# Attention scores of one row of query blocks in a two-bank PSUM tile, with one maximum, one exponential and one sum

## The chip, the cores and the metric

The kernel runs on one core of a Trainium2 chip. The metric is device time in microseconds (us) from launch to end, as the median of three runs. Times of single instructions come from one profiled execution.

## What is computed

Two layers of a decoder trunk, on 1024 tokens of width 1024, in float32. Each layer has a token-mixing sub-layer of four head groups (A, B, C, D) and a gated MLP. The change touches group C, causal softmax attention with four heads:

```python
def attend(args):                      # one block of 128 queries
    qn, qr, blk = args
    sc = (einsum('bqhd,bkhd->bhqk', qn, k_nope)
          + einsum('bqhd,bkd->bhqk', qr, k_rope)) * scale
    q_pos = blk * Q_BLOCK + arange(Q_BLOCK)
    mask = key_pos[None, :] <= q_pos[:, None]
    p = softmax(where(mask, sc, MASK_VALUE), axis=-1)
    return einsum('bhqk,bkhv->bqhv', p, v)
```

Groups A and B are gated linear recurrences, computed chunk by chunk; they share the stretch of the program with group C. Everything else of the reference is left out here, since the change does not touch it.

## The kernel before

`mixing` runs first the input projections and group D, then a stretch in which groups A, B and C are computed together, then the output projection with `w_out`. `ffn` follows. This happens once for each of the two layers. In the middle stretch, called the attention stage below, two streams are interleaved: `group_c` (32 steps, one for each head h and block t of 128 queries) and `ab` (32 steps of `gla_levels`, `gla_chunks` and the head norms of groups A, B and D). The interleaving sets the order in which the work is written; the framework's scheduler then places every instruction on its engine, and each engine keeps to that order.

PSUM has eight banks, each 512 float32 wide on 128 partitions. In the attention stage `PS2` divides them: four single-bank buffers under the tag `cs` (scores), two under `ct` (projections of q and k, transposes, outputs), two under `pm` (groups A and B).

For block t, `scores(h, t)` has (t+1)*128 keys. It is called a row below; rows t = 0 to 3 are short (at most 512 keys, one bank), rows t = 4 to 7 long (two banks). For each piece of up to 512 keys TensorE writes the products q k into one `cs` buffer (two passes of matmul for a float32 piece); on the piece with the diagonal it adds the causal mask by a bf16 matmul of `caus` with an identity. VectorE takes the maximum of each piece (L764). One `tensor_scalar` turns the maxima into the bias of the exponential (L767 for two pieces, L769 for one). ScalarE takes the exponential of each piece (L773) with its sum, which the trace shows as a second instruction, ACTIVATION_READ_ACCUMULATOR. For two pieces VectorE adds the sums (L776); then comes the reciprocal (L778). `apply(h, t)` follows two rows later (`LA = 2`): TensorE transposes P through `ct` (L219 is the transposing helper), ScalarE copies the result to `PT` (L790), TensorE multiplies by v and ScalarE scales by the reciprocal (L794). L215 is the helper that records nearly all other matmuls of the stage, so they are told apart by tiles: `cs` scores, `ct` projections and outputs, `pm` groups A and B.

Of groups A and B the lines named below are: L481 (exponential of a level), L490, L497 and L499 (masked queries of a level), L509 and L511 (copies of a level's products into `at`), L555 and L565 (output and state of a chunk), L480, L483 and L437 on GpSimd. L747 makes Q of the next head.

After the stage `cc` and `g` are closed and the buffers of the weights of `w_out` (L192) are opened in their place.

Of the kernel before, what the change touches and what calls it, by code (L numbers as in the profile page):

```python
# [12 lines left out]
AF = mybir.ActivationFunctionType  # L13
ALU = mybir.AluOpType
AX = mybir.AxisListType
# [113 lines left out]
class Body:  # L129
# [60 lines left out]
    def load(self, src, shape, pool="w", tag="wst", bufs=2):  # L190
        st = self.t(pool, tag, bufs, shape)
        self.nc.sync.dma_start(out=st, in_=src)  # L192
        return st
# [515 lines left out]
    def group_c(self, l, ckv, wv, load, krd, out):  # L709
        nc = self.nc  # L710
        small = lambda sh, tag, bufs=2, dt=F32: self.t("cc", tag, bufs, sh, dt)
        cx = lambda j: load(j, small(None, f"cx{j}", 1))
        wukv = small([128, 256], "wukv", 1)
        nc.sync.dma_start(out=wukv, in_=self.I["wukv"][l, :, 0:256])
        wuq = small([128, 2, 512], "wuq", 1)
        nc.sync.dma_start(out=wuq, in_=self.I["wuq"][l])
        cq = cx(0), cx(1)
        tab = small([128, S], "tab", 1)
        nc.sync.dma_start(out=tab, in_=self.I["tab"])
        vt = [small([128, 4, 256], f"cv{z}", 1) for z in range(2)]  # L720
        for tp in range(4):
            p = self.ps([128, 2, 256], "ct")
            for e in range(2):
                t = tp * 2 + e
                self.mm(p[:, e, :], ckv[:, t * 128:(t + 1) * 128], wv)
            nc.scalar.copy(out=vt[tp // 2][:, (tp % 2) * 2:(tp % 2) * 2 + 2, :], in_=p)

        id16 = small([128, 128], "id16", 1, BF16)
        nc.vector.tensor_copy(out=id16, in_=self.ident)
        caus = small([128, 128], "caus", 1, BF16)  # L730
        nc.vector.tensor_copy(out=caus, in_=self.cf[:, C_CAUS:C_CAUS + 128])
        scale = 96.0 ** -0.5
        QK = {}

        def head(h):
            Q = small(None, "Q", 2)
            K = small(None, "K", 2)
            nc.sync.dma_start(out=K[64:128], in_=krd)
            for n in range(2):
                sl = slice(n * 512, (n + 1) * 512)  # L740
                p = self.ps([64, 512], "ct")
                self.mm(p, wukv[:, h * 64:(h + 1) * 64], ckv[:, sl])
                nc.scalar.copy(out=K[0:64, sl], in_=p)
                p = self.ps([128, 512], "ct")
                for i in range(2):
                    self.mm(p, wuq[:, i, h * 128:(h + 1) * 128], cq[i][:, sl], i == 0, i == 1)
                nc.vector.tensor_tensor(out=Q[:, sl], in0=p, in1=tab[:, sl], op=ALU.mult)  # L747
            QK[h] = Q, K

        def scores(h, t):  # L750
            Q, K = QK[h]
            nk = (t + 1) * 128
            qc = Q[:, t * 128:(t + 1) * 128]
            ps = []
            nm = small([128, 2], "nm", 4)
            for a in range(0, nk, 512):
                e = min(nk, a + 512)
                dg = e == nk
                p = self.ps([128, 512], "cs")[:, 0:e - a]
                self.mm(p, qc, K[:, a:e], True, not dg)  # L760
                if dg:
                    self.mm(p[:, e - a - 128:e - a], id16, caus, False, True)
                i = len(ps)
                nc.vector.tensor_reduce(out=nm[:, i:i + 1], in_=p, axis=AX.X, op=ALU.max)  # L764
                ps.append(p)
            if len(ps) == 2:
                nc.vector.tensor_scalar(out=nm[:, 0:1], in0=nm[:, 0:1], scalar1=nm[:, 1:2], scalar2=-scale, op0=ALU.max, op1=ALU.mult)  # L767
            else:
                nc.vector.tensor_scalar(out=nm[:, 0:1], in0=nm[:, 0:1], scalar1=-scale, scalar2=None, op0=ALU.mult)  # L769
            P = small(None, "P", LA + 1)  # L770
            sm = small([128, 2], "sm", 4)
            for i, p in enumerate(ps):
                nc.scalar.activation(out=P[:, i * 512:i * 512 + p.shape[1]], in_=p, func=AF.Exp, scale=scale, bias=nm[:, 0:1],  # L773
                                     accum_out=sm[:, i:i + 1])
            if len(ps) == 2:
                nc.vector.tensor_tensor(out=sm[:, 0:1], in0=sm[:, 0:1], in1=sm[:, 1:2], op=ALU.add)  # L776
            rc = small([128, 1], "rc", 4)
            nc.vector.reciprocal(out=rc, in_=sm[:, 0:1])  # L778
            return P, rc

        def apply(h, t, P, rc):
            po = None
            PT = small([128, 8, 128], "PT", 2)
            for j in range((t + 4) // 4):
                n = min(4, t + 1 - j * 4)
                p = self.ps([128, 4, 128], "ct")
                for b in range(n):
                    kb = j * 4 + b
                    self.tr(p[:, b, :], P[:, kb * 128:(kb + 1) * 128])
                nc.scalar.copy(out=PT[:, j * 4:j * 4 + n, :], in_=p[:, 0:n, :])  # L790
            po = self.ps([128, 64], "ct")
            for kb in range(t + 1):
                self.mm(po, PT[:, kb, :], vt[kb // 4][:, kb % 4, h * 64:(h + 1) * 64], kb == 0, kb == t)
            nc.scalar.activation(out=out(t)[:, h * 64:(h + 1) * 64], in_=po, func=AF.Copy, scale=rc)  # L794

        head(0)
        prev = []
        for h in range(4):
            for t in range(8):
                prev.append((h, t) + scores(h, t))  # L800
                if t == 4 and h < 3:
                    head(h + 1)
                if len(prev) > LA:
                    apply(*prev.pop(0))
                yield
        for a in prev:
            apply(*a)
# [260 lines left out]
    def mixing(self, l, hT, x_src, x_dst):  # L1068
# [21 lines left out]
        self.exp_ln(self.marks["tanh"])  # L1090
        self.open_ps(**PS2)
        self.open("z", side="left")
# [573 lines left out]
NP, NU, NUL, NFIN = 10, 4, 4, 6  # L1666

LA = 2
PS2 = dict(cs=4, ct=2, pm=2)
NN = (32, 32)  # L1670

HALF = (slice(0, 2), slice(2, 4))
# [25 lines left out]
```

## Time and profile before

| what | value |
|---|---|
| median of 3 runs | 2962.63 us (2961.93 to 2962.8) |
| the profiled execution's own time | 2966.25 us |
| its span, first to last instruction | 2964.5 us |
| PE busy (share of the span) | 2746.8 us (93%) |
| DVE busy | 1868.4 us (63%) |
| ACT busy | 1272.9 us (43%) |
| POOL busy | 1211.7 us (41%) |
| attention stage, layer 0 | about 475 to 698 us |
| attention stage, layer 1 | about 1950 to 2173 us |

PE is TensorE, PEld its weight loads, DVE VectorE, ACT ScalarE, POOL GpSimd, SP the queue that issues the DMAs. Busy shares are means over stages with different limits, so the two attention stages have to be read by themselves. The profiled execution took 3.6 us longer than the median.

### The profile page before, as it was taken

To read this page: it belongs to the slowest core of one execution; us is meant where nothing else is said; L and a number is where in the kernel's file an instruction comes from. 1 tells how busy PE (TensorE), PEld (TensorE's weight loads), DVE (VectorE), ACT (ScalarE), POOL (GpSimd) and SP (SyncE) were. 2 spreads that over 40 slices of the span, in tenths; PEclk is the share of its full clock that TensorE was granted. 3 is DMA by queue.
4 is the path that set the end of the run, shared out by engine and by line. 5 is a ranking of instruction groups with operands and counts; after the bars stand their busy time and mean duration, and the time that the engine had idled before them with its cause. 6 is when DMAs were issued, how large, how long until landed. Compare 5 with 4: busy or idle time off the path is not lost. (4 is left out here: it accounts for less than half of the span.)

```text
span 2964.5 us, 40124 instructions
## 1 busy us (share of the span) xinstructions
PE 2746.8 (93%) x14928; PEld 2230.7 (75%) x14928; DVE 1868.4 (63%) x2726; ACT 1272.9 (43%) x2338; POOL 1211.7 (41%) x1030
## 2 busy tenths in 40 slices
PE   7999898899889999999979998978998999999998
PEld 6787685677777888888767876956776778888887
DVE  5564424893597777764645645258836977777645
ACT  4523335555543333354435233365545433333443
POOL 2122675444575454300231326744446654443001
PEclk9999999999999999999989999999999999999999
DMA  3221764123433223376522226741134332333765
GB/s 115 66 94 57 243 251 160 49 72 107 149 103 110 98 100 105 124 255 194 171 67 69 90 74 234 266 140 57 58 114 149 102 112 101 100 101 105 258 196 192
DMA packets 162675, 386.02 MB, mean 130 GB/s; under 512 B 25488, under 2 KB 37040, under 8 KB 162480
## 3 DMA queue, kind: packets, MB, share of 16 engines
q1 hardware_dynamic: 162480, 383.47, 38.8%
q8 instruction: 117, 1.92, 0.3%
q14 instruction: 78, 0.64, 0.1%
HBM read 273.76 MB, written 109.64 MB: 129 GB/s over the span
## 5 line engine op out<-in xcount | busy, mean ns | idle before, releaser
L209 PE MATMUL pd<-h,wr 128*128 128x512 f32 x2608 | 668.3, 406 | 29.5 <-ACT wr L197 19.8
L198 POOL TENSOR_TENSOR wr<-wst,wr 128x512 fp32r<-128x512 f32 (+1 forms) x184 | 351.1, 1910 | 750.4 <-ACT wr L197 749.2
L209 PEld LDWEIGHTS pd<-h,wr 128*128 128x128 f32 x2608 | 494.9, 192 | 150.5 <-ACT wr L197 22.3
L197 ACT CAST wr<-wst 128x512 fp32r<-128x512 f32 (+1 forms) x256 | 194.4, 762 | 337.4 <-PE pd L209 232.8
L209 PE MATMUL pd<-wr,h 128*128 128x256 f32 x1920 | 245.5, 288 | 0.7 <-DVE gt L407 0.7
L209 PE MATMUL pm<-h,wr 128*128 128x512 f32 x864 | 233.4, 397 | 9.5 <-DVE x L1397 9.5
L209 PEld LDWEIGHTS pd<-wr,h 128*128 128x128 f32 x1920 | 237.9, 196 | 2.8 <-DVE gt L407 0.9
L198 DVE TENSOR_TENSOR h<-st,h 128x1024 fp32r<-128x1024 f32 x120 | 152.6, 1273 | 123.8 <-ACT h L197 122.5
L209 PEld LDWEIGHTS pm<-h,wr 128*128 128x128 f32 x864 | 164.7, 191 | 47.6 <-DVE x L1397 10.3
L209 PE MATMUL pd<-wr,f 128*128 128x512 f32 x768 | 185.3, 398 | 11.6 <-POOL wr L198 10.6
L197 ACT CAST h<-st 128x1024 fp32r<-128x1024 f32 x120 | 125.8, 1050 | 147.9 <-PE pd L209 84.2
L209 PE MATMUL pd<-h 128*128 128x512 f32 x816 | 185.6, 389 | 0.0
L209 PEld LDWEIGHTS pd<-wr,f 128*128 128x128 f32 x768 | 143.7, 189 | 44.9 <-POOL wr L198 12.3
L209 PEld LDWEIGHTS pd<-h 128*128 128x128 f32 x816 | 153.2, 188 | 31.8
L209 PE MATMUL pm<-h 128*128 128x512 f32 x720 | 165.7, 390 | 0.8 <-DVE h L198 0.8
L1335 DVE SCALAR_TENSOR_TENSOR g<-z,pp,g 128x512 f32<-128x512 f32 x176 | 157.5, 895 | 8.2
L209 PEld LDWEIGHTS pm<-h 128*128 128x128 f32 x720 | 134.9, 188 | 29.6 <-DVE h L198 1.6
L1456 POOL TENSOR_TENSOR y<-y,gb 128x512 f32<-128x512 f32 x24 | 38.7, 1623 | 273.4 <-ACT fc L230 205.7
L215 PE MATMUL pm<-g,g 128*128 128x128 f32 (+1 forms) x672 | 119.8, 326 | 29.9 <-issue 12.9
L215 PEld LDWEIGHTS pm<-g,g 128*128 128x128 f32 x672 | 98.4, 200 | 57.3 <-issue 31.9
L209 PE MATMUL pd<-hs,wr 128*128 128x512 f32 x528 | 133.9, 405 | 5.0 <-ACT x L1401 5.0
L209 PE MATMUL pm<-hs,wr 128*128 128x512 f32 x528 | 129.8, 394 | 2.9 <-DVE hs L198 2.9
(366 smaller groups left out, 5395.8 us busy)
## 6 DMA issues: line engine op xcount, KB each, us to landing
st<-gd SPq DMA_DIRECT2D x144, 256.0 KB, 3.1
gd<-g SPq DMA_DIRECT2D x88, 256.0 KB, 2.0
d<-in_wdn_dram SPq DMA_DIRECT2D x40, 512.0 KB, 5.4
td<-d SPq DMA_DIRECT2D x40, 512.0 KB, 3.2
st<-td SPq DMA_DIRECT2D x80, 256.0 KB, 3.7
ust<-in_wgu_dram SPq DMA_DIRECT2D x36, 512.0 KB, 3.6
wst<-in_wgu_dram SPq DMA_DIRECT2D x36, 512.0 KB, 3.6
st<-in_wdn_dram SPq DMA_DIRECT2D x68, 256.0 KB, 3.2
```

Of the source, the lines that this page charges most:

```text
L197: self.marks["hi"] = self.nc.scalar.copy(out=hi, in_=src)
L198: (eng or self.nc.gpsimd).tensor_tensor(out=lo, in0=src, in1=hi.bitcast(F32), op=ALU.subtract)
L209: mm = lambda x, y, **k: self.nc.tensor.matmul(out, lhsT=x, rhs=y, skip_group_check=onto, **k)
L215: self.nc.tensor.matmul(out, lhsT=lhsT, rhs=rhs, start=start, stop=stop)
L1335: nc.vector.scalar_tensor_tensor(out=c, in0=x[:, j:j + 512], scalar=w(j), in1=c, op0=ALU.mult, op1=ALU.add)
L1456: (dve if last and n else pool).tensor_tensor(out=y[t][:, c], in0=y[t][:, c], in1=g_post[:, c], op=ALU.mult)
```

## The change

A row's scores lie in one tile of 1024 columns, two banks wide, whatever the row's length. There are two such tiles under `cs` in place of four single-bank buffers; the number of banks is the same. The matmuls are the same ones. One maximum, one exponential with one sum, and no addition serve a row; the bias always takes the one-operand form.

```diff
-            ps = []
-            nm = small([128, 2], "nm", 4)
+            p = self.ps([128, 1024], "cs")
+            nm = small([128, 1], "nm", 4)
             for a in range(0, nk, 512):
                 e = min(nk, a + 512)
                 dg = e == nk
-                p = self.ps([128, 512], "cs")[:, 0:e - a]
-                self.mm(p, qc, K[:, a:e], True, not dg)
+                self.mm(p[:, a:e], qc, K[:, a:e], True, not dg)
                 if dg:
-                    self.mm(p[:, e - a - 128:e - a], id16, caus, False, True)
-                i = len(ps)
-                nc.vector.tensor_reduce(out=nm[:, i:i + 1], in_=p, axis=AX.X, op=ALU.max)
-                ps.append(p)
-            if len(ps) == 2:
-                nc.vector.tensor_scalar(out=nm[:, 0:1], in0=nm[:, 0:1], scalar1=nm[:, 1:2], scalar2=-scale, op0=ALU.max, op1=ALU.mult)
-            else:
-                nc.vector.tensor_scalar(out=nm[:, 0:1], in0=nm[:, 0:1], scalar1=-scale, scalar2=None, op0=ALU.mult)
+                    self.mm(p[:, e - 128:e], id16, caus, False, True)
+            nc.vector.tensor_reduce(out=nm, in_=p[:, 0:nk], axis=AX.X, op=ALU.max)
+            nc.vector.tensor_scalar(out=nm, in0=nm, scalar1=-scale, scalar2=None, op0=ALU.mult)
             P = small(None, "P", LA + 1)
-            sm = small([128, 2], "sm", 4)
-            for i, p in enumerate(ps):
-                nc.scalar.activation(out=P[:, i * 512:i * 512 + p.shape[1]], in_=p, func=AF.Exp, scale=scale, bias=nm[:, 0:1],
-                                     accum_out=sm[:, i:i + 1])
-            if len(ps) == 2:
-                nc.vector.tensor_tensor(out=sm[:, 0:1], in0=sm[:, 0:1], in1=sm[:, 1:2], op=ALU.add)
+            sm = small([128, 1], "sm", 4)
+            nc.scalar.activation(out=P[:, 0:nk], in_=p[:, 0:nk], func=AF.Exp, scale=scale, bias=nm, accum_out=sm)
             rc = small([128, 1], "rc", 4)
-            nc.vector.reciprocal(out=rc, in_=sm[:, 0:1])
+            nc.vector.reciprocal(out=rc, in_=sm)
...
-PS2 = dict(cs=4, ct=2, pm=2)
+PS2 = dict(cs=2, ct=2, pm=2)
```

The scheduler also places other instructions differently. Numbers behind a name are running numbers of tiles; they differ between the two programs. In the changed program L763 is the maximum, L764 the bias, L767 the exponential, L769 the reciprocal.

VectorE, layer 0, head 0, from the third row's maximum to the fifth row's reciprocal. Before:

```order
L764 TENSOR_REDUCE nm_4155<-cs_4156 128x1
L778 RECIPROCAL rc_4116<-sm_4114 128x1
L769 TENSOR_SCALAR nm_4155<-nm_4155 128x1
L764 TENSOR_REDUCE nm_4218<-cs_4219 128x1
L778 RECIPROCAL rc_4164<-sm_4162 128x1
L769 TENSOR_SCALAR nm_4218<-nm_4218 128x1
L764 TENSOR_REDUCE nm_4287<-cs_4288 128x1
L778 RECIPROCAL rc_4227<-sm_4225 128x1
L764 TENSOR_REDUCE nm_4287<-cs_4291 128x1
L767 TENSOR_SCALAR nm_4287<-nm_4287 128x1
L776 TENSOR_TENSOR sm_4297<-sm_4297 128x1
L778 RECIPROCAL rc_4301<-sm_4297 128x1
```

With the change:

```order
L769 RECIPROCAL rc_4116<-sm_4114 128x1
L763 TENSOR_REDUCE nm_4156<-cs_4155 128x1
L764 TENSOR_SCALAR nm_4156<-nm_4156 128x1
L763 TENSOR_REDUCE nm_4219<-cs_4218 128x1
L769 RECIPROCAL rc_4164<-sm_4162 128x1
L764 TENSOR_SCALAR nm_4219<-nm_4219 128x1
L769 RECIPROCAL rc_4227<-sm_4225 128x1
L763 TENSOR_REDUCE nm_4288<-cs_4287 128x1
L764 TENSOR_SCALAR nm_4288<-nm_4288 128x1
L769 RECIPROCAL rc_4297<-sm_4295 128x1
```

The fifth row's second maximum and its addition are gone. The third row's maximum stands behind the second row's reciprocal (rc_4116), and the fifth row's behind the fourth row's (rc_4227); before, both stood ahead.

TensorE, layer 0, where the first two rows of head 1 (128 and 256 keys) follow head 0. Before:

```order
L215 MATMUL pm_4267<-g_4258,g_4238 128x256 x2
L219 MATMUL ct_4482<-cf,P_4296 128x128
L215 MATMUL cs_4574<-K_4304,Q_4303 128x128
L215 LDWEIGHTS id_611_4016
L215 MATMUL cs_4574<-caus_4018,id_611_4016 128x128
L215 MATMUL cs_4666<-K_4304,Q_4303 128x256
```

With the change:

```order
L215 MATMUL cs_4557<-K_4300,Q_4299 128x128
L215 LDWEIGHTS id_611_4016
L215 MATMUL cs_4557<-caus_4018,id_611_4016 128x128
L215 MATMUL pm_4250<-g_4245,g_4238 128x256 x2
L215 MATMUL pm_4254<-g_4245,g_4238 128x256 x2
L215 MATMUL pm_4263<-g_4258,g_4238 128x256 x2
L215 MATMUL pm_4267<-g_4258,g_4238 128x256 x2
L219 MATMUL ct_4470<-cf,P_4294 128x128
L215 MATMUL ct_4473<-cv_605_3998,PT_4463 128x64 x4
L215 MATMUL ct_4473<-cv_606_3999,PT_4463 128x64
L219 MATMUL ct_4539<-cf,P_4380 128x128 x4
L215 MATMUL cs_4649<-K_4300,Q_4299 128x256
```

The two short rows stood next to each other; now a level of group B (pm) and the transposes and outputs of two rows of head 0 (ct) stand between them.

ScalarE, layer 0, the exponential of row t = 5 of head 0. Before:

```order
L509 COPY at_4059<-pm_4150 32x8x32 x2
L497 ACTIVATE g_4180<-qm_4178,cf 128x4x64 x4
L497 ACTIVATE g_4193<-qm_4178,cf 128x4x64 x4
L481 ACTIVATE g_4238<-g_4238 128x1024
L773 ACTIVATE P_4386,sm_4387<-cs_4378,nm_4377 128x512
L773 ACTIVATE P_4386,sm_4387<-cs_4381,nm_4377 128x256
```

With the change:

```order
L509 COPY at_4057<-pm_4086 64x8x64
L481 ACTIVATE g_4118<-g_4118 128x1024
L785 ACTIVATE z_3984<-ct_4322,rc_4164 128x64
L767 ACTIVATE P_4380,sm_4381<-cs_4373,nm_4374 128x768
L509 COPY at_4058<-pm_4095 64x8x64
L509 COPY at_4059<-pm_4099 64x8x64
```

It stands two levels of group B earlier, between the copies of the first level.

## Rows read from the trace of the kernel before

**Rows 1.** The profile's page: span, and busy time of each engine with its share of the span and its instructions.

```profile
span 2964.5 us, 40124 instructions
PE 2746.8 (93%) x14928; PEld 2230.7 (75%) x14928; DVE 1868.4 (63%) x2726; ACT 1272.9 (43%) x2338; POOL 1211.7 (41%) x1030
```

**Rows 2.** Busy time in the two attention stages: stretch in us, its length, then for PE, PEld, DVE, ACT and POOL the busy us and (instructions), then granted clock, DMA share, GB/s.

```profile
475.00:698.00 223.00, 200.52 (x1218) 154.37 (x1218) 185.15 (x395) 133.31 (x346) 91.97 (x80) 0.97 0.17 56
1950.00:2173.00 223.00, 200.05 (x1198) 153.35 (x1197) 184.60 (x393) 132.02 (x342) 89.17 (x79) 0.96 0.17 55
```

**Rows 3.** What TensorE waited for in the stage of layer 0: us in total, times, longest.

```profile
PE pm L215 <- issue: 6.5, 4, 3.1
PE pm L215 <- DVE g L499: 3.3, 4, 1.0
PE ct L215 <- ACT PT L790: 2.3, 4, 0.7
...
PE pm L215 <- ACT P L773: 0.6, 1, 0.6
PE cs L215 <- ACT P L773: 0.4, 2, 0.3
```

**Rows 4.** The chain of work that ended last, in the stage of layer 1: first by line over 1949 to 2175 us, then by line over 2060 to 2175 us, then single pieces (start, us, what).

```profile
by line: PE pm L215 23.0%; PE ct L215 13.6%; PE cs L215 9.4%; DVE g L499 9.2%; DVE at L511 5.9%; issue 5.8%; PE ct L219 4.4%; ACT g L497 3.1%; DVE S L565 2.6%; DVE nm L764 2.3%; DVE qm L490 1.9%; DVE g L479 1.7%; DMA g<-Av 1.5%; ACT g L481 
...
by line: PE pm L215 26.4%; PE ct L215 16.8%; DVE g L499 10.1%; PE cs L215 9.6%; DVE at L511 6.7%; PE ct L219 5.5%; DVE S L565 4.2%; DVE nm L764 4.0%; DMA g<-Av 2.9%; DVE g L479 2.4%; DVE sm L776 2.2%; PE pm L219 1.9%; issue 1.5%; DVE hn L42
...
2006.96 0.44 DVE sm L776
...
2102.34 1.15 DVE sm L776
```

**Rows 5.** Groups of instructions by line and shape in the stage of layer 0 (475 to 698 us): line, engine, operation, out<-in, shapes, xcount | busy us, mean ns of one | idle us just before them, and what ended it.

```profile
L773 ACT ACTIVATE P<-cs,nm 128x512 f32<-128x512 f32 x24 | 16.5, 687 | 4.1 <-DVE nm L767 3.6 <-DVE nm L769 0.5
L764 DVE TENSOR_REDUCE nm<-cs 128x1 f32<-128x512 f32 x24 | 16.4, 682 | 1.3 <-PE cs L215 1.2
...
L773 ACT ACTIVATION_READ_ACCUMULATOR P<-cs,nm 128x1 f32 x48 | 9.6, 200 | 0.0
...
L776 DVE TENSOR_TENSOR sm<-sm 128x1 f32<-128x1 f32 x16 | 5.8, 360 | 2.0 <-ACT P L773 1.9
...
L764 DVE TENSOR_REDUCE nm<-cs 128x1 f32<-128x384 f32 x8 | 4.4, 551 | 0.2
...
L764 DVE TENSOR_REDUCE nm<-cs 128x1 f32<-128x256 f32 x8 | 3.4, 419 | 0.6 <-PE cs L215 0.5
L767 DVE TENSOR_SCALAR nm<-nm 128x1 f32<-128x1 f32 x16 | 3.3, 204 | 0.1
L773 ACT ACTIVATE P<-cs,nm 128x128 f32<-128x128 f32 x8 | 2.9, 363 | 4.1 <-DVE nm L769 4.1
L764 DVE TENSOR_REDUCE nm<-cs 128x1 f32<-128x128 f32 x8 | 2.3, 288 | 1.2 <-PE cs L215 1.1
L769 DVE TENSOR_SCALAR nm<-nm 128x1 f32<-128x1 f32 x16 | 2.1, 144 | 0.1
```

**Rows 6.** The stage of layer 0 in order of time around the sixth row's exponentials: start us, us, engine, line, operation, out<-in.

```profile
508.13 0.69 ACT L773 ACTIVATE P<-cs,nm 128x512 f32<-128x512 f32 x1
508.72 0.19 ACT L773 ACTIVATION_READ_ACCUMULATOR P<-cs,nm 128x1 f32 x1
508.81 0.46 ACT L773 ACTIVATE P<-cs,nm 128x256 f32<-128x256 f32 x1
...
509.26 1.30 ACT L497 ACTIVATE g<-qm,cf 128x256 f32<-128x256 f32 x3
...
509.92 1.04 POOL L480 TENSOR_TENSOR g<-g 128x512 f32<-128x512 f32 x1
...
509.96 1.02 DVE L776 TENSOR_TENSOR sm<-sm 128x1 f32<-128x1 f32 x1
510.90 0.68 DVE L764 TENSOR_REDUCE nm<-cs 128x1 f32<-128x512 f32 x1
```

**Rows 7.** The first rows of head 0, layer 0, in order of time (columns as in rows 6).

```profile
475.63 0.86 PE L215 MATMUL cs<-K,Q 128*128 128x384 f32 x2
475.81 0.37 ACT L773 ACTIVATE P<-cs,nm 128x128 f32<-128x128 f32 x1 [4.09 <-DVE nm L769]
...
476.59 0.56 DVE L764 TENSOR_REDUCE nm<-cs 128x1 f32<-128x384 f32 x1
...
477.20 0.17 DVE L778 RECIPROCAL rc<-sm 128x1 f32<-128x1 f32 x1
```

**Rows 8.** The short rows of head 1, layer 0: the matmuls of rows t = 2 and 3 and the exponentials of rows t = 0 and 1 (columns as in rows 6).

```profile
524.95 0.81 PE L215 MATMUL cs<-K,Q 128*128 128x384 f32 x2
...
530.22 0.36 ACT L773 ACTIVATE P<-cs,nm 128x128 f32<-128x128 f32 x1
...
533.79 1.02 PE L215 MATMUL cs<-K,Q 128*128 128x512 f32 x2
...
540.68 0.46 ACT L773 ACTIVATE P<-cs,nm 128x256 f32<-128x256 f32 x1
```

**Rows 9.** The end of the stage of layer 0: the last scaling of an attention output, the first loads of `w_out`, the first long run of the output projection (columns as in rows 6).

```profile
697.08 0.32 ACT L794 ACTIVATE z<-ct,rc 128x64 f32<-128x64 f32 x1 [0.72 <-PE ct L215]
...
697.42 0.81 SPq L192 DMA_DIRECT2D wst<-in_wo_dram  x2
...
705.94 43.34 PEld L209 LDWEIGHTS pd<-wr,f 128*128 128x128 f32 x189 [1.90 <-POOL wr L198]
```

## The prediction

> **What bounds the kernel now.** I read the page first, then the busy times of the two attention stages, then TensorE's waits there, and last the chain of work that ended last. Over the whole span TensorE is busy 93% and VectorE 63% [rows 1], so the kernel as a whole is TensorE's. The change touches two stretches of 223 us, and these look different: TensorE is busy 200.5 us and VectorE 185.2 us of 223 in layer 0, and nearly the same in layer 1 [rows 2]. ScalarE has 133 us and GpSimd 92 us. TensorE thus has 223 - 200.5 = 22.5 us of idle time in a stage, which is the most that a better order could give back there. Its waits are many and short; the longest with a name end in L499 of groups A and B on VectorE and in the copy PT on ScalarE [rows 3]. The chain shows why: in the stage of layer 1 it changes all the time between TensorE (matmuls of pm, ct and cs) and VectorE (L499, L511, L565 of groups A and B), and the attention's own maxima (L764) and additions (L776) stand between these on VectorE, which works in order [rows 4]. So the stage is held by TensorE and VectorE in turns, and part of what the change removes lies on that path.
>
> What the stage's end is worth: the last scaling of an attention output runs at 697.08 us, the loads of w_out are issued at 697.42 and the output projection gets going at 705.94 [rows 9]. Those loads need the space that the stage gives free, so a stage that ends earlier or later by some time moves everything behind it by the same. Both layers have the same order, so what holds for one is counted twice.
>
> **The change part by part, for one layer.** There are 16 long rows (4 heads, t = 4 to 7).
>
> *Additions removed.* 16 additions L776 of one element take 5.8 us, 360 ns each [rows 5], though the bias, of one element too, takes 144 ns. One of them shows why the mean is high: it starts at 509.96, takes 1.02 us and ends together with a GpSimd instruction that ran from 509.92 for 1.04 us [rows 6]. The next VectorE instruction, a maximum that reads PSUM, begins at once and does not wait in the same way, so I count such waiting as removed and not as passed on. On the chain the additions have 2.2% of the 115 us from 2060 to 2175, which is 2.5 us, and 0.44 us at 2006.96 [rows 4]. I take 2.9 us.
>
> *Maxima joined.* The mean maximum takes 288, 419, 551 and 682 ns for 128, 256, 384 and 512 columns [rows 5]: about 131 ns for each 128 columns, and 157 ns that do not depend on the columns. A joined row saves 157 ns, 16 x 0.157 = 2.5 us of busy time. No row of the trace shows a read over two banks; at worst it takes what the two parts take together and saves nothing, at best 0.16 us. I take the 0.16, since the four shapes lie on one line. Maxima fill 16.4 + 4.4 + 3.4 + 2.3 = 26.5 us [rows 5] and have 2.3% of 226 us, 5.2 us, on the chain [rows 4]. The joined ones shorten this by 2.5/26.5 of 5.2, or 0.5 us.
>
> *Bias.* The form with two scalars takes 204 ns, that with one 144 [rows 5]: 16 x 0.06 = 1.0 us busy, and with the chain share of the maxima (5.2/26.5) 0.2 us.
>
> *Exponentials joined.* 363 ns for 128 columns and 687 for 512 [rows 5] make 108 ns for each 128 and 255 fixed, and each carries a read of the sum of 200 ns. These overlap: from 508.13 to 508.81 to 509.26 the next one starts 0.68 us after 512 columns and 0.45 after 256 [rows 6], so 0.22 us are fixed in terms of when the next can start. One fewer saves between 0.22 and 0.455 us, 3.5 to 7.3 us of ScalarE for a layer; I take 3.5, since the start of the next instruction is what counts. ScalarE is busy 133 of 223 us and TensorE waits for exponentials only 0.6 + 0.4 us [rows 3], so nearly all of this hides behind other engines; I count 0.3 us.
>
> The gains on the path are 2.9 + 0.5 + 0.2 + 0.3 = 3.9 us. The bounds: nothing, if TensorE fills the path wherever VectorE leaves it; and all of VectorE's removed work, 5.8 + 2.5 + 1.0 = 9.3 us, if VectorE alone sets the pace.
>
> The Trainium skill has fixed costs for these instructions (Perfetto Trace Analysis, Optimizing Scalar/DVE Operations: about 125 ns on VectorE and 51 ns on ScalarE for data in PSUM, with the profiled duration showing about twice that). By that page the maxima would give 16 x 0.125 = 2.0 us of busy time and the exponentials 16 x 0.051 = 0.8 us, an estimate; the sum would be smaller by some 0.3 us a layer, and I keep to the rows.
>
> *Two tiles where there were four buffers.* A long row had two of four buffers and now has one of two, which is the same. A short row had one of four and now has one of two, so its matmul must wait until the row two places ahead has had its exponential. At the start of the stage this shows: the third row's matmul ran at 475.63, but the first row's exponential ends only at 475.81 + 0.37 = 476.18 [rows 7]. And VectorE's new order puts the third row's maximum behind the second row's reciprocal, which ended at 477.20 + 0.17 = 477.37, while the maximum began at 476.59 [rows 7]. That is 0.55 to 0.78 us, in a place with little else to do; I count 0.7 us lost. In heads 1 to 3 the order sets other matmuls between the short rows, and I count nothing: the cover there is a level of group B and the outputs of the head before.
>
> *Whole rows.* The maximum can no longer begin while the second piece is multiplied, and the transposes wait for the whole exponential. VectorE waited 1.2 us before its 512-column maxima for scores [rows 5], and TensorE 1.0 us for exponentials [rows 3]. If each such wait grows by half, 0.5 us are lost. What is late next in that case is the row's transposes, which stand two rows behind and mostly have time.
>
> *Moved.* The exponential of the sixth row now stands between two copies of the first level of group B and delays the second of them; before, it stood ahead of an L497 of a later level and ran right before it [rows 6]. I count the two as even. GpSimd's queue keeps its instructions and moves only some dv products of L554 by a place; SP's moves a load of K ahead of a load of a gate, and two loads of x by a place. One issue on SP takes 0.4 us (two in 0.81 us [rows 9]), so I count nothing there.
>
> Sum: 3.9 - 0.7 - 0.5 = 2.7 us a layer, 5.4 us in all. The terms come from the profiled execution, whose own time of 2966.25 us lies 3.6 us above the median; a difference carries over. Against the median, 2962.6 - 5.4 = **2957.2 us**. A difference of 0.2%, 5.9 us, is what a measurement of this kernel can tell from none, so my forecast is a small gain near that edge, most likely within it.
>
> **The rivals.**
> *TensorE takes the path over.* TensorE is busy 200.5 of 223 us [rows 2], and where VectorE is shortened the matmuls beside it may become the path. For it speaks the share of pm, ct and cs in the chain, over half [rows 4]; against it, that the additions stand on the chain with nothing beside them. Then the 3.9 us shrink to about 1.2 and the losses eat them: 2961 to 2964 us.
>
> *VectorE sets the pace throughout.* Then all 9.3 us count, less the 1.2 lost: 8.1 a layer, 16.2 in all, 2946.4 us. For it: 185 of 223 us busy, and additions that GpSimd waits for; against it, the chain has TensorE in more than half of its length.
>
> *The ring of two stalls TensorE (slower).* In head 1 the matmul of the third row ran at 524.95 and that of the fourth at 533.79, while the exponentials of the first and second ran only at 530.22 and 540.68 [rows 8]: with two tiles these matmuls could not have run then. If the new order places them where the exponential is late, TensorE stands still with all that is queued behind. At one exponential of about 0.7 us [rows 5] for each of the 12 short rows of heads 1 to 3, a layer loses 8.4 + 1.2 us against 3.9 gained, 5.7 net, and the kernel takes 2962.6 + 11.4 = 2974 us. It decides from about 8 stalled rows a layer, where the loss passes the gain by over 3 us. Against it: the new order has a whole level of group B between two short rows. The Trainium skill speaks for it, and so against this change (Perfetto Trace Analysis, Matmul Optimizations: see that all eight PSUM banks are used so that instructions can run side by side); half of the rows would leave the second bank of their tile empty.
>
> **How the numbers follow.** Forecast, 2953 to 2961 us: 0.47. TensorE takes over: 0.16. VectorE throughout: 0.17. Ring: 0.20. Faster by over 0.2% are the case of VectorE and the part of the forecast below 2956.7, somewhat less than half of it, 0.21: 0.38. Within 0.2% are the rest of the forecast and TensorE's case: 0.42. Slower: 0.20. The range leaves out the far ends of VectorE's case and of the ring's, a tenth each: 2947 to 2971 us. The forecast's own range is 2953 to 2961.
>
> **What would show it.** In the profile after, each layer should have 16 fewer maxima and exponentials, with the longest about 1.21 us (157 + 8 x 131 ns) and 1.12 us (255 + 8 x 108 ns), and no additions; VectorE's busy time in the stage should fall by about 9 us and ScalarE's by 3.5 to 7; the last scaling of an attention output should come about 2.7 us earlier counted from the stage's start. A maximum of 1.36 us would show that two banks cost what two reads cost. Waits of TensorE for exponentials before cs matmuls, well over the 0.4 us of now, would show the ring. A stage that keeps its length with VectorE 9 us less busy would show TensorE's case. The prediction is wrong if the stage gets longer, or shorter by over 5 us a layer.

## The result and the profile after

The changed kernel takes 2983.92 us (median of 6 runs, 2978.32 to 2988.01), the kernel before 2963.98 us beside it: ratio 1.0063, 95% interval 1.0052 to 1.0074. It is 0.63% slower, some 19 us. The prediction had 2957.2 us and 0.2 for slower. In a second comparison the ratio was 1.0069 (1.0053 to 1.0085).

The page of the changed kernel, to be read beside [rows 1]; its profiled execution took 2988.0 us:

```profile
span 2986.2 us, 39998 instructions
PE 2762.6 (93%) x14928; PEld 2246.4 (75%) x14928; DVE 1858.9 (62%) x2662; ACT 1264.0 (42%) x2274; POOL 1210.8 (41%) x1030
```

VectorE and ScalarE have less to do, by 9.5 and 8.9 us, and the span is 21.7 us longer. The two attention stages, from the first scores to the last scaled output, with the columns of [rows 2]:

```profile
474.50:706.60 232.10, 203.93 (x1213) 158.54 (x1213) 183.68 (x366) 128.93 (x314) 92.69 (x81) 0.95 0.16 52
1964.90:2198.10 233.20, 205.60 (x1213) 160.20 (x1213) 183.26 (x366) 128.73 (x314) 91.39 (x80) 0.94 0.17 53
```

The stages of before, measured in the same way:

```profile
474.74:697.40 222.66, 200.23 (x1213) 154.08 (x1213) 184.94 (x394) 133.22 (x346) 91.37 (x80) 0.97 0.17 57
1949.80:2175.32 225.52, 202.22 (x1213) 155.39 (x1213) 185.83 (x394) 133.11 (x346) 90.30 (x80) 0.96 0.17 55
```

So 9.4 and 7.7 us, 17 of the 21.7, are lost here. Two things stand in these rows. The granted clock of TensorE is 0.95 and 0.94, against 0.97 and 0.96. And the time that TensorE does not work (length less busy time) grew from 22.4 and 23.3 us to 28.2 and 27.6. Between the two stages another 5.9 us are lost, 1258.3 us against 1252.4; a run in the same order (h6 below) has 1254.0 there, and what makes this difference stays open.

The groups of maxima, exponentials and small operations in the stage of layer 0, which answer to [rows 5]:

```profile
L499 DVE SCALAR_TENSOR_TENSOR g<-g,cf,g 128x512 f32<-128x512 f32 x28 | 36.7, 1334 | 1.2 <-ACT g L481 1.1
...
L763 DVE TENSOR_REDUCE nm<-cs 128x1 f32<-128x1024 f32 x4 | 4.9, 1220 | 0.8 <-PE cs L215 0.8
L769 DVE RECIPROCAL rc<-sm 128x1 f32<-128x1 f32 x32 | 4.9, 157 | 5.1 <-ACT P L767 5.0
...
L767 ACT ACTIVATE P<-cs,nm 128x1024 f32<-128x1024 f32 x4 | 4.4, 1112 | 3.8 <-DVE nm L764 3.8
```

The joined maximum over 1024 columns takes 1.22 us and the joined exponential 1.11 us; forecast were 1.21 and 1.12. The reciprocals now wait 5.0 us for exponentials. L499, which the change does not touch, takes 1334 ns on average; before it took 1170, so 28 of them take 4.6 us more:

```profile
L499 DVE SCALAR_TENSOR_TENSOR g<-g,cf,g 128x512 f32<-128x512 f32 x28 | 32.2, 1170 | 1.4 <-ACT g L481 1.4
```

What TensorE waits for in the stage of layer 0 (columns as in [rows 3]), and behind it one line of before:

```profile
PE pm L215 <- DVE g L499: 5.6, 5, 2.7
PE pm L215 <- ACT kT L560: 5.3, 2, 3.3
PE cs L215 <- ACT P L767: 3.2, 3, 1.4
```

```profile
PE pm L215 <- ACT kT L560: 0.6, 1, 0.6
```

Waits of scores for exponentials, the sign named for the ring, grew from 0.4 to 3.2 us. But the waits for L499 and for kT (L560, a copy of groups A and B; 0.6 us before) grew by 2.3 and 4.7 us, and neither is part of the change.

The end of the stage of layer 0 (columns as in [rows 9]):

```profile
706.24 0.31 ACT L785 ACTIVATE z<-ct,rc 128x64 f32<-128x64 f32 x1 [1.37 <-PE ct L215]
...
706.58 0.81 SPq L192 DMA_DIRECT2D wst<-in_wo_dram  x2
...
714.10 21.00 PEld L209 LDWEIGHTS pd<-wr,f 128*128 128x128 f32 x92 [1.66 <-POOL wr L198]
```

The loads of w_out follow the last scaling by 0.34 us, as before. The last scaling comes 9.2 us later than before, and the first long run of the output projection 8.2 us later (714.10 against 705.94 [rows 9]).

### The profile page after: what moved, and what is told of

It is laid out like the page before. It is cut to its first block, busy times and chain, and to the rows that moved or that the text cites. A ratio compares the mean times of both kernels' runs of the same rounds, so it can differ in the third digit from the quotient of the medians.

```text
span 2986.2 us, 39998 instructions
## 1 busy us (share of the span) xinstructions
PE 2762.6 (93%) x14928; PEld 2246.4 (75%) x14928; DVE 1858.9 (62%) x2662; ACT 1264.0 (42%) x2274; POOL 1210.8 (41%) x1030
## 5 line engine op out<-in xcount | busy, mean ns | idle before, releaser
L209 PE MATMUL pd<-h,wr 128*128 128x512 f32 x2608 | 668.4, 406 | 27.6 <-ACT wr L197 18.1
L215 PE MATMUL pm<-g,g 128*128 128x128 f32 (+1 forms) x672 | 125.5, 338 | 29.9 <-issue 14.2
L215 PEld LDWEIGHTS pm<-g,g 128*128 128x128 f32 x672 | 103.7, 209 | 54.7 <-issue 25.1
```

The lines of the kernel that those rows point to most:

```text
L209: mm = lambda x, y, **k: self.nc.tensor.matmul(out, lhsT=x, rhs=y, skip_group_check=onto, **k)
L215: self.nc.tensor.matmul(out, lhsT=lhsT, rhs=rhs, start=start, stop=stop)
```

## The experiments

Three theories were tried. **Ring**: only two rows, short ones too, fit in two two-bank tiles. **Whole rows**: a joined operation makes others wait for all of a row. **Order**: with other operations and buffers the scheduler finds another order for every engine, and that order costs. Where a run adds code, its line numbers are higher by some lines: L217 in h2 is the helper L215, L775 there the exponential. Each run was timed against the kernel before on the same chip:

| run | operations | places for short rows | order | ratio (95% interval) |
|---|---|---|---|---|
| changed kernel | joined | 2 | own | 1.0063 (1.0052 to 1.0074) |
| e0_pairs_split | split | 2 tiles, shared in pairs | own | 1.0064 (1.0046 to 1.0082) |
| e1_ring_split | split | 2 | own | 1.0118 (1.0105 to 1.0131) |
| e2_joined_pairs | joined | 2 tiles, shared in pairs | own | 1.0063 (1.0049 to 1.0077) |
| e3_three_buffers | split | 3 | own | 1.0017 (1.0009 to 1.0026) |
| f1_two_places_split | split | 2 for each piece | own | 1.0045 (1.0032 to 1.0058) |
| f2_four_places_joined | joined | 4, opened anew | own | 1.0082 (1.0067 to 1.0097) |
| f3_order_swap | split | 4 | other | 1.0063 (1.0048 to 1.0079) |
| f4_order_head | split | 4 | other | 1.0065 (1.0046 to 1.0084) |
| g1_split_after_order | split | 4 | of the change | 1.0052 (1.0037 to 1.0066) |
| h3_joined_after_order | joined | 4, in pairs | of the change | 1.0037 (1.0023 to 1.0052) |
| h6_bank_after_order | joined | 4, bank by bank | of the change | 1.0040 (1.0025 to 1.0054) |
| h2_joined_before_order | joined | 4, in pairs | of before | 1.0043 (1.0030 to 1.0055) |
| h4_bank_before_order | joined | 4, bank by bank | of before | 0.9999 (0.9987 to 1.0010) |
| g3_no_add_before_order | split, no addition | 4 | of before | 1.0008 (0.9998 to 1.0018) |
| h1_joined_free_order | joined | 4, in pairs | own | 1.0010 (0.9997 to 1.0023) |
| h5_bank_own_order | joined | 4, bank by bank | own | 1.0008 (0.9998 to 1.0018) |
| i1_one_copy_earlier | joined | 2 | of the change, one copy moved | 1.0067 (1.0051 to 1.0084) |
| i0_after_again | joined | 2 | own | 1.0069 (1.0053 to 1.0085) |

**Ring or joining, each alone.** e0 and e1 keep the split operations in two two-bank tiles, e2 joins them; e3 takes one buffer away.

```diff
 e1 (e0 and e2: a new tile only for t > 3 or even t, odd short rows in its second half)
+            two = self.ps([128, 1024], "cs")
-                p = self.ps([128, 512], "cs")[:, 0:e - a]
+                p = two[:, a:e]
-PS2 = dict(cs=4, ct=2, pm=2)
+PS2 = dict(cs=2, ct=2, pm=2)
 e3
-PS2 = dict(cs=4, ct=2, pm=2)
+PS2 = dict(cs=3, ct=2, pm=2)
```

> A control: maxima, exponentials, sums and additions stay split in pieces as before, and the banks in use are as before, but they are asked for as two two-bank tiles: two short rows share one tile (one bank each), a long row has one. Ring theory (two short rows no longer fit where four did): the time of the kernel before, 2961 to 2967 us, since four short rows still fit. Whole-row theory (the joined maximum and exponential make others wait): the same, since nothing is joined. Order theory (the scheduler's other placing of the instructions is what costs): it may land anywhere between 2955 and 2990, since the placing changes as much as in the changed kernel.

> Only the ring of two: maxima, exponentials, sums and additions stay split as before, but every row, short ones too, takes one of two two-bank tiles. Ring theory: all of the loss and none of the gain, 2984 to 2992 us, with cs matmuls waiting for exponentials by over 5 us a layer. Whole-row theory: 2961 to 2969 us, as before but for 0.7 us a layer. Order theory: anywhere between 2955 and 2990.

> The changed kernel's joined maximum, exponential and sum, but two short rows share a two-bank tile, one bank each, so that four short rows fit as before. Ring theory: the gain without the loss, 2955 to 2962 us. Whole-row theory: the loss stays, 2978 to 2986 us. Order theory: anywhere between 2955 and 2990.

> The kernel before with three single-bank buffers for scores in place of four and nothing else changed (one bank stays unused). Ring theory: fewer rows in flight cost time here too, less than with two places for short rows: 2968 to 2980 us. Whole-row theory: 2961 to 2967 us. Order theory: anywhere between 2955 and 2990.

Ring and whole rows both expected the time of before for e0, which has four places and joins nothing; it is 0.64% slower. But the trace of e0 shows a flaw of the design, here at the first two rows of head 0 (columns as in [rows 7]):

```profile
477.05 0.37 ACT L777 ACTIVATE P<-cs,nm 128x128 f32<-128x128 f32 x1 [4.37 <-DVE nm L773]
...
477.56 0.70 PE L215 MATMUL cs<-K,Q 128*128 128x256 f32 x2 [0.31 <-ACT P L777]
```

The second row's matmul writes the other bank of the tile, and yet waits for the first row's exponential. The framework treats the two banks of one tile as one, so e0, e1 and e2 have waits of their own and settle nothing. e3 has none of these waits and loses 0.17%.

f1 gives first and second pieces single-bank buffers of their own; f2 opens the buffers anew for each four rows.

```diff
 f1
+                p = self.ps([128, 512], "cs" if a == 0 else "c2")[:, 0:e - a]
+PS2 = dict(cs=2, c2=2, ct=2, pm=2)
 f2
+            if t % 4 == 0:
+                ...
+                self.open("sc", space=PSUM)
+            p = self.t("sc", "cs", 2 if t > 3 else 4, [128, 1024 if t > 3 else 512])
 f3
-        streams = [self.group_c(l, *cx, at(oc)), ab()]
+        streams = [ab(), self.group_c(l, *cx, at(oc))]
 f4
-                if t == 4 and h < 3:
+                if t == 3 and h < 3:
```

> The ring of two alone, in single banks: the first piece of a row takes one of two buffers, the second piece one of two others, so only two rows fit, short or long, as in the changed kernel; maxima, exponentials, sums and additions stay split as before, and no piece waits for the other's maximum as in the earlier run with split pieces in two-bank tiles. Ring theory: the whole loss and none of the gain, 2982 to 2992 us. Whole-row theory: 2961 to 2969 us. Order theory: anywhere between 2960 and 2990.

> The joined operations with four places for short rows: the buffers for scores are opened anew after each four rows, as four single banks for the short rows and as two two-bank tiles for the long ones. At each of these seven changes a layer the first row waits for the exponential of the row before it. Ring theory: most of the loss is gone, 2958 to 2970 us. Whole-row theory: the loss stays, 2978 to 2986 us. Order theory: anywhere between 2960 and 2990.

> The kernel before with the two interleaved streams begun in the other order (a step of groups A and B is written ahead of each row of scores, not behind it); the same instructions, buffers and operations. Ring theory and whole-row theory: 2961 to 2969 us, as nothing of theirs is touched. Order theory: a difference of 8 to 25 us from before in either direction, as large as the change's own.

> The kernel before with the projections of the next head written one row earlier (behind the fourth row, not the fifth); the same instructions, buffers and operations. Ring theory and whole-row theory: 2961 to 2969 us. Order theory: a difference of 8 to 25 us from before in either direction.

f3 and f4 decide here. They change nothing but the order in which work is written, and they cost 0.63 and 0.65%, as much as the change. Another order alone can thus cost this much. It need not: h1 and h5 below are joined, run in new orders of their own, and lie 0.10 and 0.08% above before, which their intervals do not tell from nothing. A loss or gain of a program in its own order (f1, f2, e3) cannot then be put down to its buffers. f1, at 0.45%, lies between what ring and whole rows expected of it, f2, at 0.82%, above what either expected; they settle nothing.

**The order held fixed.** In these runs a table holds every engine's instructions in a given order. In the h runs two short rows share a tile and the framework's waits between its banks are left out (h1 to h3), or all scores lie in one four-bank tile and a bank waits for its own users alone (h4 to h6).

```diff
+    for line in zlib.decompress(base64.b64decode(ORDER)).decode().split("\n"):
+        ...
+        for a, b in zip(names, names[1:]):
+            tc.add_manual_dep(ins[b], a, info, reason="order")
 h4, h5, h6
+            b = t if t < 4 else t % 2 * 2
+            p = four[:, b * 512:b * 512 + 1024 if t > 3 else b * 512 + 512]
 g3
-                nc.vector.tensor_tensor(out=sm[:, 0:1], in0=sm[:, 0:1], in1=sm[:, 1:2], op=ALU.add)
```

> The kernel before, with split operations and four single-bank buffers, but every engine's instructions are held in the order that they have in the changed kernel (the second maximum and exponential right beside the first, the addition ahead of the reciprocal). Order theory: the loss is in the order, so 2980 to 2992 us although no row has two banks and nothing is joined. Ring theory and whole-row theory: 2961 to 2967 us, since neither two places nor whole-row operations are there.

> The changed kernel's joined operations in the changed kernel's order on every engine, but with four places for short rows (two short rows share a two-bank tile, and the waits that the framework would set between the two banks of one tile are left out). Only the waits for a free tile differ from the changed kernel. Order theory: 2978 to 2986 us, as the changed kernel. Ring theory: 2955 to 2966 us, since the waits for a tile are gone. Whole-row theory: 2978 to 2986 us.

> Joined operations with four places for short rows, and every engine's instructions held in the order of the kernel before (the joined maximum where the second piece's stood, the joined exponential where the first piece's stood, no addition). Order theory: the gain of the prediction's sum without a new order, 3.9 us a layer less at most 0.5 for whole rows: 2955 to 2961 us. Ring theory: the same. Whole-row theory: 2975 to 2986 us.

> Joined operations with four places for short rows as in the two runs beside it, but in the order that the scheduler finds by itself for this program. Order theory: anywhere between 2960 and 2995 us, most likely slower than before by 10 us or more. Ring theory: 2955 to 2962 us. Whole-row theory: 2978 to 2986 us.

g1 has no joined operation and no two-bank tile, only the order of the change, and loses 0.52%. h1 missed what the order theory held likeliest, a loss of 10 us or more: 0.10% are 3 us. h2 was a surprise: 0.43% lost in the order of before. TensorE's scores and ScalarE's exponentials in head 1, layer 0, of h2:

```profile
543.24 2.08 PE L217 MATMUL cs<-K,Q 128*128 128x512 f32 x2 [4.85 <-ACT P L775]
...
556.61 1.12 PE L217 MATMUL cs<-K,Q 128*128 128x512 f32 x2 [2.02 <-ACT P L775]
```

```profile
542.63 0.46 ACT L775 ACTIVATE P<-cs,nm 128x256 f32<-128x256 f32 x1
...
555.77 0.70 ACT L775 ACTIVATE P<-cs,nm 128x512 f32<-128x512 f32 x1
```

The first matmul of a long row waits for the second of the two short rows that share its tile (256 columns, done at 543.09; 512 columns, done at 556.47): 6.9 us a layer that single banks do not cost. Up to there the rows run within 1 us of before. That asked for the runs bank by bank.

> Joined operations, all scores of a layer in one four-bank tile: short rows take banks 0 to 3 in turn, long rows banks 0 and 1 or 2 and 3, and a bank waits only for the rows that used that bank. Every engine is held in the order of the kernel before. In the earlier run in that order, two long rows of head 1 waited 4.8 and 2.0 us a layer for a whole tile; the first of these waits is gone here. If such tile waits were that run's whole loss, 2957 to 2966 us, and the joined operations' gain shows as up to 3.9 us a layer; if joined operations cost time in this order by themselves (whole-row theory), 2972 to 2982 us.

> The same program with the four-bank tile, every engine held in the order of the changed kernel: the changed kernel without any wait for a two-bank tile. If the order carries the larger part of the loss and waits for tiles the rest, 2974 to 2981 us, as in the earlier run with pairs of short rows in this order (2979.1). If tiles carry it all, 2957 to 2966 us. If neither the order nor tiles but the joining, 2980 to 2988 us.

> The kernel before in its own order, with the 16 additions a layer left out and nothing else changed (the reciprocal takes the sum of the last piece alone, so the long rows are scaled by a part of their sum). The prediction's term, 2.9 us a layer on the path: 2958 to 2963 us, 5.8 us below before. If TensorE fills what VectorE leaves (the rival in which TensorE takes over): 2963 to 2967 us, no difference. If VectorE alone sets the pace, 5.8 us a layer: 2952 to 2957 us.

> The program with the four-bank tile and joined operations in the order that the scheduler finds for it. Order theory: anywhere between 2960 and 2990 us, since the placing is new again. Ring theory: 2955 to 2963 us, better than before by the joined operations' gain. Whole-row theory: 2978 to 2986 us.

h4 and h6 are one program in two orders: 0.9999 and 1.0040. The order is worth 0.41%, some 12 us (0.22 to 0.60%, an estimate from the two intervals). h4 is joined, in the order of before, and its scores wait for exponentials only 0.7 us in the stage of layer 0. It takes the time of before to within 0.13%, though its VectorE is busy 23 us less [rows 1]. Its page, and its two stages (columns as in [rows 2]):

```profile
span 2967.1 us, 40010 instructions
...
PE 2754.3 (93%) x14928; PEld 2237.7 (75%) x14928; DVE 1845.1 (62%) x2662; ACT 1266.6 (43%) x2274; POOL 1209.0 (41%) x1030
```

```profile
473.89:698.28 224.39, 200.89 (x1213) 154.11 (x1213) 179.09 (x362) 129.67 (x314) 91.66 (x80) 0.97 0.17 54
1954.97:2178.27 223.30, 201.82 (x1213) 155.08 (x1213) 178.57 (x362) 129.84 (x314) 92.12 (x80) 0.96 0.17 54
```

The two stages of h4 last 447.7 us together, those of h6 460.0 (rows in the last section): the 12 us lie here. TensorE stands idle 45.0 us in the two of h4 and 56.4 in those of h6, so most of what the order costs is waiting of TensorE. The kernel before has 45.7 us of it, the changed kernel 55.8.

g3 agrees: without the additions nothing is gained. The changed kernel lies 0.23 to 0.29% above h6, which has the same order on every engine and differs from it by the waits for tiles alone; an interval for the difference, worked out from those of the two, just leaves zero out. No version beats the kernel before: h1, h4 and h5 equal it. No run has two tiles in the order of before, and by the rows of before none could. There the fourth row's scores of head 1 (533.79 [rows 8]) stand on TensorE ahead of transposes (534.81) whose copy PT (540.22) stands on ScalarE ahead of the second row's exponential (540.68 [rows 8]). With two tiles those scores would wait for that exponential, and so for themselves.

**One place.** TensorE's longest wait for kT in the changed kernel, with ScalarE:

```profile
639.33 0.80 PE L215 MATMUL pm<-g,kT 128*128 128x128 f32 x2 [3.35 <-ACT kT L560]
```

```profile
637.93 1.06 ACT L481 ACTIVATE g<-g 128x1024 f32<-128x1024 f32 x1 [4.06 <-DVE rc L769]
639.01 0.27 ACT L560 COPY kT<-pm 128x128 f32<-128x128 f32 x1
```

The copy stands behind an L481 that waits for VectorE; in the order of before it stands ahead of it. i1 moves it ahead, in each layer, by an edit of the table.

> The changed kernel in its own order, but for one place in each layer: on ScalarE one copy kT (L560) stands one instruction earlier, ahead of an exponential L481, as in the kernel before. In the changed kernel this copy stood behind that L481, which waited 4.06 us for VectorE, and TensorE waited 3.35 us for the copy; the granted clock then fell to half for some microseconds. If the order is what costs, the place is worth 1.5 to 3.4 us a layer and, where the clock no longer falls behind it, 1.7 to 3.4 us more: 2970 to 2981 us, against 2984 for the changed kernel. If the order does not matter, 2982 to 2988 us.

> The changed kernel itself, beside the run with one copy moved, on the same chip: every theory expects 2980 to 2988 us, 0.5 to 0.75% above before.

This missed: 1.0067 against 1.0069. The trace of i1 shows why (L501 there is L499, L562 is L560):

```profile
627.92 4.63 DVE L501 SCALAR_TENSOR_TENSOR g<-g,cf,g 128x512 f32<-128x512 f32 x2 [0.34 <-ACT g L483]
...
630.45 0.27 ACT L562 COPY kT<-pm 128x128 f32<-128x128 f32 x1 [0.42 <-PE pm L221]
...
634.58 0.27 DVE L557 TENSOR_TENSOR z<-pm,dv 128x128 f32<-128x128 f32 x1
...
635.00 2.05 PE L217 MATMUL pm<-g,g 128*128 128x128 f32 x8 [2.63 <-DVE z L557]
```

The copy now runs at once, and TensorE waits 2.63 us for VectorE's z instead, which stands behind two L499 of 4.63 us together. At this place VectorE is late, and the copy only handed that on. Which rows of the order cost how much stays open; that the order as a whole carries the larger part is shown.

## Why the prediction was wrong

*Moved.* This step failed, with the largest part. It weighed one moved exponential, counted it as even and some DMA issues at nothing; the pieces of order that it had at hand were read for the ring alone. The new order costs 0.40 to 0.52%, 12 to 15 us (h6, g1), most of it as waiting of TensorE.

*Two tiles where there were four buffers.* At the start of the stage the 0.7 us came as counted; in heads 1 to 3, counted at nothing, TensorE waits. The first and the fourth row's scores of head 0, before in layer 0, and of the changed kernel in layer 1 and in layer 0:

```profile
474.74 0.46 PE L215 MATMUL cs<-K,Q 128*128 128x128 f32 x2 [0.87 <-DMA K<-kr]
...
476.51 1.02 PE L215 MATMUL cs<-K,Q 128*128 128x512 f32 x2
```

```profile
1964.86 0.46 PE L215 MATMUL cs<-K,Q 128*128 128x128 f32 x2 [1.59 <-DMA K<-kr]
...
1967.36 1.11 PE L215 MATMUL cs<-K,Q 128*128 128x512 f32 x2
```

```profile
474.52 0.78 PE L215 MATMUL cs<-K,Q 128*128 128x128 f32 x2 [2.89 <-DVE Q L747]
...
478.23 1.91 PE L215 MATMUL cs<-K,Q 128*128 128x512 f32 x2
```

The fourth row follows the first by 1.77 us before, by 2.50 in layer 1 of the changed kernel, so 0.73 us are lost; i0, the changed kernel again, has 2.49 in layer 0. In layer 0 of the execution shown it is 3.71 us, but there the matmuls themselves are slower (0.78 us against 0.46 for the same shape). Behind a wait of 2.89 us the granted clock was 0.58 and then 0.50 (columns as in [rows 2]):

```profile
474.00:476.00 2.00, 1.48 (x5) 1.23 (x6) 1.49 (x4) 0.04 (x1) 0.00 (x0) 0.58 1.03 412
476.00:478.00 2.00, 2.00 (x5) 0.74 (x4) 0.78 (x4) 0.98 (x4) 0.00 (x0) 0.50 1.02 406
```

In layer 1 it was 1.00 at this place, as before the change. So what is over 0.7 us is the clock of one execution and not the ring. Two of the waits in a later head:

```profile
618.71 1.35 PE L215 MATMUL cs<-K,Q 128*128 128x512 f32 x4 [1.37 <-ACT P L767]
...
627.21 1.12 PE L215 MATMUL cs<-K,Q 128*128 128x512 f32 x2 [1.44 <-ACT P L767]
```

In all the waits for tiles cost 0.23 to 0.29%, 7 to 9 us for both layers; 1.2 us a layer had been allowed for tiles and whole rows together. In the traces they do not show as more idle time: TensorE idles 55.8 us in the stages of the changed kernel and 56.4 in those of h6, and the first are 5.3 us longer at a granted clock of 0.95 and 0.94 against 0.97 and 0.95. How the one leads to the other is not shown. The rival of the ring had this mechanism, and its 2974 us lie nearer to the measured time than the forecast; that is in part luck, as it put the whole loss down to the ring, which is less than half of it. (Its 8 stalled rows come to 2.9 us net, 8 x 0.7 + 1.2 - 3.9, and not to over 3.) The Trainium skill's advice to keep all eight PSUM banks in use (Perfetto Trace Analysis, Matmul Optimizations) points the same way; the difference between the changed kernel and h6 is its price here.

*Additions, maxima, bias, exponentials.* Durations were right, their worth was not. The 3.9 us a layer became nothing (h4, between -3.9 and +3.0 us for both layers; g3 for the additions alone). The share of a line in the chain was read as time that goes when the line goes. In h4 that time went to other things: its stages last 224.4 and 223.3 us, against 222.7 and 225.5, though VectorE is 5.9 and 7.3 us less busy in them. That is the sign that was named for the rival in which TensorE takes over, and its bound, nothing, was in the text.

*Whole rows.* Not measured apart. Half of the two waits that were named (1.2 and 1.0 us) is 1.1 us, where 0.5 were counted. h4 has them, and with the gains they come to nothing, within the bounds above. Part of what was forecast is there: VectorE waits 4.9 us for scores in the stage of layer 0 of h4, against 2.7 before.

*VectorE's busy time.* 9.3 us a layer were to go; 4.8 went. Most of the rest came back in L499, 4.6 us in layer 0 and 3.7 in layer 1. The last section has more on this.

## What to carry to other kernels

Where a scheduler sets the order, an edit is two edits: what it changes and a new order. Price the second one by changing nothing but the order, two or three times, and hold the order fixed to read the first. Here new orders cost from nothing (h1, h5) to 0.65%, the joined operations nothing, and two tiles in place of four buffers 0.23 to 0.29%. A share in the chain of waits is not what goes with a line: here it promised 3.9 us a layer and nothing came. And a tile that spans two banks was freed as one (e0, h2). Before a slow stretch of one execution is put down to the edit, look at the granted clock there, and at a second execution.

## What the runs showed of the hardware

Most L499 take longer beside GpSimd. At 562.50 in the changed kernel GpSimd is idle, and two of them take 1.41 us; at 565.72 two take 4.62, beside GpSimd instructions:

```profile
562.50 1.41 DVE L499 SCALAR_TENSOR_TENSOR g<-g,cf,g 128x512 f32<-128x512 f32 x2
...
565.72 4.62 DVE L499 SCALAR_TENSOR_TENSOR g<-g,cf,g 128x512 f32<-128x512 f32 x2 [0.42 <-ACT g L481]
565.76 1.28 POOL L483 TENSOR_TENSOR g<-g,g 128x512 f32<-128x512 f32 x1 [3.76 <-ACT g L481]
566.99 2.80 POOL L525 TENSOR_TENSOR g<-g,g 128x1024 f32<-128x1024 f32 x1
```

In the stage of layer 0 the five that have no GpSimd instruction beside them take 0.74 to 0.75 us each; of the other 23 six take up to 0.84 us and 17 over 1 us. So the order also sets how long VectorE's instructions last: the mean is 1.33 us in h6 and 1.26 in h4, one program in two orders. The Trainium skill says that the two engines share a read port of SBUF (Perfetto Trace Analysis, Optimizing Scalar/DVE Operations); these rows agree, as does the slow addition of [rows 6].

The granted clock adds to what a pause costs. Here is the changed kernel behind the wait for kT, in steps of 2 us (columns as in [rows 2]):

```profile
636.00:638.00 2.00, 0.00 (x0) 0.00 (x0) 2.00 (x4) 0.07 (x1) 1.27 (x1) 1.00 0.00 0
638.00:640.00 2.00, 0.67 (x3) 0.67 (x4) 1.65 (x4) 1.63 (x3) 1.25 (x2) 0.54 0.00 0
640.00:642.00 2.00, 2.00 (x12) 2.00 (x11) 2.00 (x2) 0.00 (x0) 0.88 (x1) 0.50 0.00 0
642.00:644.00 2.00, 2.00 (x11) 2.00 (x11) 1.52 (x5) 0.42 (x2) 0.00 (x0) 0.50 0.00 0
644.00:646.00 2.00, 2.00 (x16) 2.00 (x15) 0.60 (x1) 1.37 (x3) 0.56 (x1) 0.75 0.00 0
```

TensorE stood still and then worked for over 5 us at the lower of its two levels (0.50, 1.2 of 2.4 GHz). Not every fall in the stages follows a pause as long as this one, so the rows show the sequence and not the rule. Counting a stage's length times what its clock lacks of 1, the stages of before lost 6.7 and 9.0 us to it and those of the changed kernel 11.6 and 14.0. That is an estimate, and it counts stretches in which TensorE stood idle too. By busy time the same 1213 matmuls take 3.7 and 3.4 us longer, and TensorE idles 5.7 and 4.3 us longer. Of the 17 us that the stages grew, some 7 are thus slower matmuls and 10 waiting. The clock is also why one order gives two lengths. The two stages of h6, with the same order:

```profile
475.10:702.50 227.40, 199.31 (x1213) 154.94 (x1213) 182.69 (x366) 128.55 (x314) 92.69 (x80) 0.97 0.17 54
1956.50:2189.10 232.60, 204.25 (x1213) 158.98 (x1213) 183.36 (x365) 128.63 (x314) 92.72 (x80) 0.95 0.17 53
```

They differ by 5.2 us, while TensorE is idle 28.1 us in one and 28.4 in the other. The same 1213 matmuls are busy 4.9 us longer in the second; by the count above the clock took 6.8 us in the first, at 0.97, and 11.6 in the second, at 0.95.
